# Seven products of quarters in the last layer's up-projection, two of their weight sums added by the DMA, and modulation work and token differences respaced

## The chip, the core and the metric

One core of one Trainium2 chip runs the whole program; the other cores are idle. The metric is the device time of one execution in microseconds, as the median over several runs. PE is TensorE, the matmul engine; PEld its weight loads; DVE is VectorE, ACT is ScalarE, POOL is GpSimd and SP is SyncE, which here only issues DMAs.

## What is computed

Two layers (DEPTH = 2) of a hybrid block run on 512 latent tokens and 256 context tokens, 1024 features wide. The second layer needs the context only for its keys, values and states, so everything behind its mixing works on the 512 latent tokens alone. Cut to what matters here:

```python
mod_x = silu(c) @ w_mod[l] + b_mod[l]            # 6 x 1024 numbers; mod_c the same from c_ctx
sh1, sc1, gt1, sh2, sc2, gt2 = split(mod_x, 6)
h = rmsnorm(x, g1) * (1 + sc1) + sh1
x = x + gt1 * (concat(conv(h), window_attention(h), gla(h)) @ w_out)
h = rmsnorm(x, g2) * (1 + sc2) + sh2
a, b = split(h @ w_up, 2)                        # w_up: 1024 x 5632, so a and b are 2816 wide
x = x + gt2 * ((silu(a) * b) @ w_down)           # the FFN; then the context the same in layer 0
```

Everything is float32 in and out.

## The kernel before

**Precision.** Each float32 operand of a large matmul is split into a high part (a cast on ACT) and a low part (a subtraction on DVE), and each product is three matmul passes, high by high, high by low and low by high. In the program's names `whi` and `wlo` are tiles that hold split weights (or, in the units below, one tile that holds both halves), `act` are tiles of the split tokens, `raw` is a weight slot as it was loaded, `t` is a temporary, `main` and `bank` are PSUM banks.

**Weights.** A list `plan`, written out ahead (L424 to L494), holds every weight load of the kernel in order: keys such as ("o2", m) for the out-projection, ("a", f) and ("b", f) for the two 1024 x 128 pieces of the up-projection that make 128 features f of the FFN (f = 0 to 21), ("d", bi, m) for the down-projection of block bi. SP loads them (`w_load`, L505, DMA at L519) into a ring of four slots of 512 KB; a load waits until the slot's former content has been read. `w_advance` (L523) splits weights ahead of their use, and `w_next` (L555) hands them out.

**Modulation.** The rows of `w_mod` go through the same ring, as items that `mod_items` (L362) scatters between the others: (layer, group, ...) for 12 groups of 512 features in each layer. Groups 4 to 8 of layer 0 are items (half, kk) of four matmuls each on TensorE (`mod_step`, L639, `bank<-raw,cst`), and a group ends with a copy, four transposes and a sum. All later groups are items q on VectorE (`mod_step_v`, L673): for each of two rows of an item, a multiply-add over 512 columns (`t<-raw,cst,t`) per condition, and after the fourth item a transpose, a sum and a small matmul per condition. There are two conditions (tokens and context), but only one where the last layer needs the tokens alone (its groups 4 to 11).

**The order of instructions.** A planner keeps an estimate of each engine's clock. The main line of the program issues matmuls, and whenever the estimated PE clock passes a task's ready time, that task's next step is issued (`S.poll`, L294). The engines then run their queues in that order. What an engine has been given first it does first, whatever waits behind it.

**The FFN** (L1910 on) runs in blocks of f (`F_BLOCKS`: 5, 5, 4, 4, 4 in layer 0 and 6, 6, 6, 4 in layer 1): the up-projection of the block's f, then the block's share of the down-projection, m = 0 to 7. The features f = 0 and 1 come from `Firsts` (L768), which starts while the norm of the tokens is still being made.

In layer 0 the other twenty f are `Unit`s (L1073). The weights of f and the tokens are each cut into two by two quarters, and seven products of sums of quarters (p1 to p7, table `SEVEN`, L1069) take the place of eight: with the row of `a` as first weight row, the row of `b` as second, and the left and right half of the tokens as columns. A product is 4 x 3 = 12 matmuls over half the tokens (384 columns in layer 0). The sums of token quarters (t1 to t4) are made once per layer by `Quartered.differences` (L1039), the sums of weight quarters (s1 to s4) per f by `Unit.make` (L1082) on VectorE, each followed by its split. `run_units` (L1192) makes a product's weights when the product four places ahead of it has run, and `Opened` (L740) starts the first two down-projections before the last f is ready. `Firsts.run` calls `hook`, which begins the first unit, before its last part.

In layer 1 the twenty f went through `dense_pass` (L722): two passes per f, of 8 x 3 = 24 matmuls each over all 512 tokens.

## Time and profile before

| | |
|---|---|
| median of 3 runs | 1634.88 us (1633.03 to 1636.54) |
| the profiled execution, its own time | 1632.85 us |
| its span in the trace | 1630.9 us |
| granted TensorE clock, mean | 0.995 |
| PE busy | 1586.0 us, 97% of the span |
| DVE busy | 1149.9 us, 71% |
| ACT busy | 681.1 us, 42% |
| POOL busy | 35.8 us, 2% |
| moved by DMA | 168.45 MB, 103 GB/s in the mean |

Busy times are sums over an engine's instructions, where an instruction that starts before the one ahead of it has ended counts in full; distances between starts tell an engine's pace better. A span of 1630.9 us and a time of 1632.85 us leave 1.95 us around the span.

### The profile page before, as it was taken

The numbers are of one execution on the slowest core, as the hardware profiler recorded it, in microseconds if no ns is written. First come the engines' busy times: TensorE is split into PE (matmuls) and PEld (weight loads), VectorE is DVE, ScalarE is ACT, GpSimd is POOL, SyncE is SP. The second block draws the span as 40 slices with busy tenths as digits, with TensorE's granted clock in tenths as the row PEclk, the third lists the DMA queues.
The fourth block names the chain that finished last, engine by engine and source line by source line (L and its number), as shares of the span: only waits on it lengthen the run. The fifth ranks groups of instructions, "written<-read, shape, count | busy, mean of one in ns | idle before, by whom it ended". The sixth has DMA issues, their size and how long they took to land.

```text
span 1630.9 us, 26988 instructions
## 1 busy us (share of the span) xinstructions
PE 1586.0 (97%) x10786; PEld 1370.5 (84%) x10786; DVE 1149.9 (71%) x2212; ACT 681.1 (42%) x1374; POOL 35.8 (2%) x58
## 2 busy tenths in 40 slices
PE   7999999999999999999999999998999999999998
PEld 6878777887888899998989988786889888888887
DVE  5587876669899998878788676979787433333336
ACT  4445544453653243241423535455464322222224
POOL 2000000000000000000000000000000000000002
PEclk9999999999999999999999999999999999999999
DMA  9831312243223544526354332211222333233322
GB/s 260 248 102 26 92 53 78 67 168 103 80 78 111 161 117 122 162 80 193 98 158 122 87 105 68 50 39 46 77 75 77 88 93 105 84 110 91 101 80 78
DMA packets 252670, 168.45 MB, mean 103 GB/s; under 512 B 29828, under 2 KB 233088, under 8 KB 252544
## 3 DMA queue, kind: packets, MB, share of 16 engines
q1 hardware_dynamic: 248960, 155.93, 33.2%
q0 software_dynamic: 1760, 5.47, 1.1%
q10 hardware_dynamic: 1824, 5.31, 0.9%
q8 instruction: 85, 1.39, 0.4%
q14 instruction: 41, 0.34, 0.1%
HBM read 159.35 MB, written 7.34 MB: 102 GB/s over the span
## 4 chain that ended last, share of the span: by engine, by line
PE 79%; DVE 10%; ACT 2%; DMA 1%; issue 1%; SPq 0%; DVEq 0%; ACTq 0%
PE main L139 58%; PE bank L139 19%; DVE act L188 3%; PE bank L143 3%; DVE t L188 1%; DVE wlo L188 1%; DVE t L199 1%; ACT t L155 1%; DMA raw<-in_w_mod_dram 1%; DVE t L216 1%; ACT t L177 1%; DVE mx L207 1%; DVE t L193 0%; DMA raw<-in_w_out_dram 0%; ACT whi L177 0%
## 5 line engine op out<-in xcount | busy, mean ns | idle before, releaser
L139 PE MATMUL main<-act,whi 128*128 128x512 f32 (+2 forms) x2976 | 812.8, 364 | 1.8 <-ACT act L155 1.3
L139 PEld LDWEIGHTS main<-act,whi 128*128 128x128 f32 x2976 | 530.1, 189 | 83.7 <-issue 9.1
L139 PE MATMUL main<-act,wlo 128*128 128x512 f32 (+2 forms) x1728 | 547.3, 358 | 7.5 <-DVE wlo L188 6.5
L177 ACT CAST whi<-raw 128x1024 fp32r<-128x1024 f32 (+4 forms) x222 | 186.8, 841 | 426.8 <-PE main L139 357.8
L139 PEld LDWEIGHTS main<-act,wlo 128*128 128x128 f32 x1728 | 319.1, 188 | 48.7 <-DVE wlo L188 8.7
L188 DVE TENSOR_TENSOR wlo<-raw,whi 128x1024 fp32r<-128x1024 f32 (+4 forms) x162 | 171.7, 1060 | 102.8 <-ACT whi L177 99.7
L199 DVE SCALAR_TENSOR_TENSOR act<-main,mods,act 128x512 f32<-128x512 f32 (+1 forms) x166 | 101.4, 613 | 76.8 <-PE main L139 75.7
L139 PE MATMUL bank<-act,whi 128*128 128x384 f32 (+4 forms) x736 | 153.5, 319 | 0.0
L139 PE MATMUL bank<-act,wlo 128*128 128x384 f32 (+4 forms) x548 | 127.5, 328 | 2.5 <-ACT wlo L177 2.2
L139 PEld LDWEIGHTS bank<-act,whi 128*128 128x128 f32 (+1 forms) x736 | 124.5, 187 | 4.5 <-DVE whi L188 0.2
L199 DVE SCALAR_TENSOR_TENSOR t<-raw,cst,t 128x512 f32<-128x512 f32 x154 | 110.2, 745 | 9.0 <-DMA raw<-in_w_mod_dram 8.4
L139 PEld LDWEIGHTS bank<-act,wlo 128*128 128x128 f32 (+1 forms) x548 | 98.8, 189 | 6.1 <-ACT wlo L177 2.5
L155 ACT ACTIVATE t<-bank,nm 128x256 f32<-128x256 f32 (+1 forms) x144 | 69.8, 497 | 60.0 <-DVE nm L199 55.3
L188 DVE TENSOR_TENSOR t<-main,t 128x512 f32<-128x512 f32 (+2 forms) x53 | 32.7, 617 | 77.1 <-PE main L139 77.0
L139 PE MATMUL main<-act 128*128 128x256 f32 (+1 forms) x516 | 81.6, 312 | 3.8 <-ACT act L177 2.3
L139 PEld LDWEIGHTS main<-act 128*128 128x128 f32 x516 | 71.6, 193 | 10.3 <-ACT act L177 2.9
L139 PE MATMUL main<-t,whi 128*128 128x256 f32 (+1 forms) x296 | 74.3, 338 | 0.0
L177 ACT COPY t<-bank 128x512 f32<-128x512 f32 (+3 forms) x109 | 48.9, 465 | 60.0 <-PE bank L139 32.0
L188 DVE TENSOR_TENSOR t<-t,t 128x256 f32<-128x256 f32 (+4 forms) x102 | 62.3, 615 | 13.4 <-ACT t L155 12.7
L188 DVE TENSOR_TENSOR act<-t,act 128x512 fp32r<-128x512 f32 (+7 forms) x94 | 67.2, 725 | 6.3 <-ACT act L177 4.3
L188 DVE TENSOR_TENSOR act<-act 128x768 f32<-128x768 f32 (+7 forms) x84 | 65.4, 790 | 1.3 <-ACT t L177 1.1
L207 DVE TENSOR_REDUCE mx<-bank 128x2 f32<-128x512 f32 (+2 forms) x104 | 56.3, 562 | 14.2 <-PE bank L139 13.7
(158 smaller groups left out, 1770.7 us busy)
## 6 DMA issues: line engine op xcount, KB each, us to landing
raw<-in_w_mod_dram SPq DMA_DIRECT2D x92, 512.0 KB, 4.1
raw<-in_w_up_dram SPq DMA_DIRECT2D x80, 512.0 KB, 3.9
raw<-in_w_in_dram SPq DMA_DIRECT2D x26, 512.0 KB, 3.9
raw<-in_w_down_dram SPq DMA_DIRECT2D x24, 384.0 KB, 3.5
raw<-in_w_down_dram SPq DMA_DIRECT2D x32, 256.0 KB, 3.1
raw<-in_w_down_dram SPq DMA_DIRECT2D x16, 320.0 KB, 3.6
raw<-in_w_in_dram SPq DMA_DIRECT2D x16, 256.0 KB, 3.7
raw<-in_w_out_dram SPq DMA_DIRECT2D x16, 256.0 KB, 3.0
```

Of the source, the lines that this page charges most:

```text
L139: self.pin("pe", self.nc.tensor.matmul(out, lhsT, rhs, start=start, stop=stop, **kw))
L143: self.pin("pe", self.nc.tensor.transpose(out, in_, ident))
L155: ins = self.pin("act", self.nc.scalar.activation(out, in_, func, **kw))
L177: self.pin("act", self.nc.scalar.copy(out, in_))
L188: self.pin(eng, self._v(eng).tensor_tensor(out, a, b, op))
L199: self.pin(eng, self._v(eng).scalar_tensor_tensor(out, a, s, b, op0, op1))
L207: self.pin("dve", self.nc.vector.tensor_reduce(out, in_, AX.X, op))
L216: self.pin("dve", self.nc.vector.copy_predicated(out, mask, data))
```

## The change

The units of layer 0 are now used for the last layer's f = 2 to 21 too, over halves of 256 tokens. Two of the sums of weight quarters (s1, and the inner sum of s2 and s3) are then made by accumulating DMAs from POOL: one loads a quarter into a temporary, one adds a second quarter to it, one adds a quarter to a slot that SP has loaded. Layer 0's groups 10 and 11 move from VectorE to TensorE, the groups of layer 1 come in another order (4 to 11, then 0 to 3), and the items lie at other places: fewer around the out-projection, two per f up to f = 13. The token differences are started inside `Firsts.run`, and layer 1's down-projection uses `Opened`.

```diff
@@ plan @@
     mod_todo = [(0, g, half, kk) for g in range(4, 9) for half in range(2) for kk in range(2)]
-    mod_todo += [(l, g, q) for l in range(DEPTH) for g in range(0 if l else 9, 12) for q in range(4)]
+    mod_todo += [(0, 9, q) for q in range(4)]
+    mod_todo += [(0, g, half, kk) for g in range(10, 12) for half in range(2) for kk in range(2)]
+    mod_todo += [(1, g, q) for g in (*range(4, 12), *range(4)) for q in range(4)]
...
             out2_item(l, m, m >= N_OUT2)
             if l == 0 and m == 0:
-                mod_items(2)
+                mod_items(1)
...
-                    w_item((l, nm, f), 8, cols(w_up[l, :, c0:c0 + P], 8), quarters=l == 0)
+                    w_item((l, nm, f), 8, cols(w_up[l, :, c0:c0 + P], 8), quarters=True)
+                    plan[-1]["sums"] = (l, f) if l and half else None
                 if l == 0:
-                    mod_items(2 if f < 4 else 1)
+                    mod_items(2 if f < 14 else 1)
...
-                plan[-1]["late"] = l == 0 and m == 1
+                plan[-1]["late"] = m == 1
                 if l == 0 and bi < len(blocks) - 1:
-                    mod_items((0, 1, 2, 2, 1, 1, 1, 0)[m])
+                    mod_items(((0, 1, 1, 2, 1, 1, 1, 0), (0, 1, 0, 1, 0, 1, 1, 0))[bi > 1][m])
@@ w_load @@
             at["dma"] += 1
+            if not it["mod"] and it["sums"]:
+                l, f = it["sums"]
+                def quarter(i, j):
+                    c0 = (i - 1) * FF + f * P
+                    return w_up[l, (j - 1) * 512:j * 512, c0:c0 + P].rearrange("(k p) n -> p k n", p=P)
+                S.room(t3=1)
+                it["sum"] = tmp()
+                e = it["sum"][:, :512].rearrange("p (k n) -> p k n", k=4)
+                S.pin("pool", nc.gpsimd.dma_start(e, quarter(2, 1)))
+                S.pin("pool", nc.gpsimd.dma_start(e, quarter(2, 2), accum_op=ALU.add))
+                S.pin("pool", nc.gpsimd.dma_start(it["raw"][:, :4, :], quarter(1, 1), accum_op=ALU.add))
+                it["t"] += 4000.0
@@ mod_step @@
         S.acopy(ms[:, :512], pm)
+        S.last += 1000
@@ Firsts.run @@
             self.weights(3)
+            if hook:
+                hook[0]()
             part(a, 2)
...
             if hook:
-                hook()
+                hook[1]()
             part(b, 3)
@@ Unit.make @@
-            if name == "s1":
+            if name == "s1" and self.ib["sums"]:
+                e = self.ib["sum"]
+                src = e[:, :512]
+            elif name == "s1":
...
             elif name == "s2":
-                S.tt(R["a21"], R["a11"], R["a21"], ALU.add)
+                if not self.ib["sums"]:
+                    S.tt(R["a21"], R["a11"], R["a21"], ALU.add)
@@ the FFN @@
-        norm = Normed(l, V_N2, 4, 3) if last else Quartered(l, V_N2, 4, 3, n)
+        norm = Quartered(l, V_N2, 4, 3, n)
...
-                if not last:
-                    diff = S.spawn(norm.differences(("t1", "t2", "t3")), prio=-1,
-                                   when=lambda: S.clk["pe"] if norm.done.get(gb, 0) == NK else None)
+                def hook0():
+                    diff.append(S.spawn(norm.differences(("t1", "t2", "t3")), prio=-1,
+                                        when=lambda: S.clk["pe"] if norm.done.get(gb, 0) == NK else None))
                 Firsts((l, "up"), (ga, gb)).run(norm, lambda i, s, pt: evs[i % 2]("ab"[i // 2], s, pt),
-                                                None if last else hook)
+                                                (hook0, lambda: begin(range(2, f1))))
...
-            if last:
-                X = norm.X()
-                for f in range(max(f0, 2), f1):
-                    S.room(t3=1, act=1)
-                    sil = tmp()
-                    ev_ab = swiglu(sil, act_t(F32R))
-                    for nm in ("a", "b"):
-                        dense_pass([(nm, *w_next((l, nm, f)), 0)], X, sg, ev_ab)
-                    S.gave(sil)
-            else:
-                heads = []
...
             tail(keys, ts_, 5, N_DOWN, lambda s, sums: fin.append(S.spawn(final_task(s, sums), prio=-2)), (ga, gb),
-                 tiles_)
+                 tiles_, opened)
```

The differences also find other places for t1 to t3 where half the tokens are 256 (`Quartered.at`).

**The first place: VectorE in layer 0's out-projection, where the hold weights of m = 1 to 7 are split** (`act<-raw,act` is the low part of such a weight; `t<-raw,cst,t` is a modulation step; `act<-main,mods,act` adds a product to the tokens). Before:

```order
L212 STREAM_TRANSPOSE t_4579<-t_4291 128x512
L199 SCALAR_TENSOR_TENSOR t_4539<-raw,cst,t_4539 128x512
L188 TENSOR_TENSOR act<-raw,act 128x512
L207 TENSOR_REDUCE part<-t_4579 128x16
L199 SCALAR_TENSOR_TENSOR t_4540<-raw,cst,t_4540 128x512
L199 SCALAR_TENSOR_TENSOR t_4539<-raw,cst,t_4539 128x512
...
L199 SCALAR_TENSOR_TENSOR t_4540<-raw,cst,t_4540 128x512
L188 TENSOR_TENSOR act<-raw,act 128x512
```

In the change:

```order
L188 TENSOR_TENSOR act<-raw,act 128x512
L199 SCALAR_TENSOR_TENSOR act<-main,mods_136,act 128x512
L212 STREAM_TRANSPOSE t_4576<-t_4291 128x512
L199 SCALAR_TENSOR_TENSOR act<-main,mods_136,act 128x256
L207 TENSOR_REDUCE part<-t_4576 128x16
L188 TENSOR_TENSOR act<-raw,act 128x512
L212 STREAM_TRANSPOSE t_4611<-t_4292 128x512
L188 TENSOR_TENSOR act<-raw,act 128x512
L207 TENSOR_REDUCE part<-t_4611 128x16
```

Between the first and the second low part of a hold weight stood a sum and seven modulation steps; now there stand two additions to the tokens, a transpose and a sum.

**The second place: VectorE in layer 0's first block of units** (`whi<-raw,whi` and `wlo<-raw,wlo` are the low parts of a product's weights, `t<-bank,t` takes a product out of PSUM). Before:

```order
L188 TENSOR_TENSOR mods_136<-bank,bmod 128x8
L188 TENSOR_TENSOR t_5467<-bank,t_5467 128x384
L199 SCALAR_TENSOR_TENSOR t_5379<-raw,cst,t_5379 128x512
L199 SCALAR_TENSOR_TENSOR t_5380<-raw,cst,t_5380 128x512
...
L188 TENSOR_TENSOR wlo<-raw,wlo 128x512
L188 TENSOR_TENSOR t_5467<-bank,t_5467 128x384
L188 TENSOR_TENSOR t_5585<-raw 128x512
```

In the change:

```order
L188 TENSOR_TENSOR t_5453<-bank,t_5453 128x384
L188 TENSOR_TENSOR wlo<-raw,wlo 128x512
L188 TENSOR_TENSOR t_5572<-raw 128x512
L188 TENSOR_TENSOR t_5453<-bank,t_5453 128x384
L188 TENSOR_TENSOR raw<-raw 128x512
L188 TENSOR_TENSOR whi<-t_5572,whi 128x512
```

Eight modulation steps stood ahead of that low part; none stands there now.

**The third place: POOL from the last layer's up-projection on.** Nothing but the final scaling stood there. In the change, after the loads of the tokens, once for each f (L535 loads a quarter, L536 adds one to it, L537 adds one to the slot):

```order
L535 DMA t_14501<-in_w_up_dram 128x4x128
L536 DMA t_14501<-in_w_up_dram 128x4x128
L537 DMA raw<-in_w_up_dram 128x4x128
L535 DMA t_14634<-in_w_up_dram 128x4x128
L536 DMA t_14634<-in_w_up_dram 128x4x128
L537 DMA raw<-in_w_up_dram 128x4x128
```

## Rows read from the trace of the kernel before

**Rows 1.** The page: busy time of the engines that matter, and the chain of work that ended last, as shares of the span by engine.

```profile
PE 1586.0 (97%) x10786; PEld 1370.5 (84%) x10786; DVE 1149.9 (71%) x2212; ACT 681.1 (42%) x1374; POOL 35.8 (2%) x58
PE 79%; DVE 10%; ACT 2%; DMA 1%; issue 1%; SPq 0%; DVEq 0%; ACTq 0%
```

**Rows 2.** Windows: the start of the program, one unit of layer 0 (seven products of 384 columns), and layer 1's up- and down-projection. Columns: stretch, its length, busy us (and count) of PE, PEld, DVE, ACT, POOL, granted clock, share of the 16 DMA engines, GB/s.

```profile
0.00:25.00 25.00, 15.95 (x134) 12.44 (x135) 11.96 (x36) 13.75 (x29) 8.78 (x24) 0.98 1.00 269
681.00:695.56 14.56, 14.56 (x86) 14.56 (x86) 10.63 (x18) 6.35 (x12) 0.00 (x0) 1.00 0.38 109
1277.00:1600.00 323.00, 323.00 (x1452) 268.13 (x1451) 119.17 (x137) 90.23 (x114) 0.00 (x0) 1.00 0.32 93
```

**Rows 3.** PE's timeline (start us, us, engine, line, operation, out<-in, shape, count) at three widths: layer 1's up-projection with 512 columns (a pair of high-weight matmuls comes every third matmul, and from the first of these rows to the second it is 30 such turns, 90 matmuls), a stretch of 92 matmuls of 256 columns in layer 1's out-projection and what follows it, and two products of a unit with 384 columns.

```profile
1440.66 0.62 PE L139 MATMUL main<-act,whi 128*128 128x512 f32 x2
...
1461.06 0.62 PE L139 MATMUL main<-act,whi 128*128 128x512 f32 x2
...
1234.76 11.20 PE L139 MATMUL main<-act 128*128 128x256 f32 x92
1245.80 0.50 PE L139 MATMUL bank<-ones,t 128*128 128x1 f32 x4
...
682.90 2.24 PE L139 MATMUL main<-act,wlo 128*128 128x384 f32 x12
684.98 2.24 PE L139 MATMUL bank<-act,whi 128*128 128x384 f32 x12
```

**Rows 4.** PE's timeline: the stretches of layer 0's out-projection and FFN that begin with a wait. In brackets the idle time before, and what ended it.

```profile
395.92 0.73 PE L139 MATMUL main<-act 128*128 128x512 f32 x2 [1.21 <-ACT act L177]
397.15 2.99 PE L139 MATMUL main<-act 128*128 128x512 f32 x12 [0.49 <-DVE act L188]
401.25 0.73 PE L139 MATMUL main<-act 128*128 128x512 f32 x2 [1.11 <-ACT act L177]
402.98 7.20 PE L139 MATMUL main<-act 128*128 128x512 f32 x24 [0.99 <-DVE act L188]
...
483.94 0.61 PE L139 MATMUL bank<-act,wlo 128*128 128x384 f32 x2 [2.16 <-ACT wlo L177]
484.88 3.42 PE L139 MATMUL bank<-act,wlo 128*128 128x384 f32 x10 [0.33 <-DVE wlo L188]
...
500.45 0.62 PE L139 MATMUL main<-act,wlo 128*128 128x384 f32 x2 [1.05 <-ACT wlo L177]
502.85 2.02 PE L139 MATMUL main<-act,wlo 128*128 128x384 f32 x10 [1.78 <-DVE wlo L188]
...
748.13 0.50 PE L139 MATMUL main<-act,wlo 128*128 128x512 f32 x1 [1.72 <-DVE wlo L188]
...
842.30 0.50 PE L139 MATMUL main<-act,wlo 128*128 128x512 f32 x1 [1.02 <-DVE wlo L188]
```

**Rows 5.** Windows just behind the first two of these places; columns as in rows 2.

```profile
403.00:406.40 3.40, 3.40 (x9) 2.70 (x10) 2.98 (x5) 1.32 (x3) 0.00 (x0) 0.55 0.54 148
485.00:488.40 3.40, 3.40 (x12) 3.40 (x13) 3.40 (x7) 0.21 (x2) 0.00 (x0) 0.56 0.00 0
```

**Rows 6.** DVE's timeline: the runs of modulation steps ahead of the low parts that PE waits for at 402 us and 502 us, the weight sum ahead of the low part at 484 us, and the idle time in layer 1's first up-projection.

```profile
397.60 4.72 DVE L199 SCALAR_TENSOR_TENSOR t<-raw,cst,t 128x512 f32<-128x512 f32 x7
402.24 0.68 DVE L188 TENSOR_TENSOR act<-raw,act 128x512 fp32r<-128x512 f32 x1
...
481.89 0.70 DVE L212 STREAM_TRANSPOSE t<-t 128x512 f32<-128x512 f32 x1
482.52 0.65 DVE L188 TENSOR_TENSOR t<-raw 128x512 f32<-128x512 f32 x1
...
496.81 5.38 DVE L199 SCALAR_TENSOR_TENSOR t<-raw,cst,t 128x512 f32<-128x512 f32 x8
502.11 0.68 DVE L188 TENSOR_TENSOR wlo<-raw,wlo 128x512 fp32r<-128x512 f32 x1
...
1278.40 1.23 DVE L188 TENSOR_TENSOR wlo<-raw,whi 128x1024 fp32r<-128x1024 f32 x1 [6.26 <-ACT whi L177]
```

**Rows 7.** PE's timeline: one modulation item on TensorE between other matmuls, and the four transposes that end a group.

```profile
348.34 0.28 PE L139 MATMUL main<-act,wlo 128*128 128x256 f32 x1
348.55 0.64 PE L139 MATMUL bank<-raw,cst 128*32 128x256 f32 x8
349.12 1.09 PE L139 MATMUL bank<-act 128*128 128x256 f32 x6
...
354.23 1.03 PE L143 MATMUL bank<-tab,t 128*128 128x128 f32 x8
355.02 0.48 PE L139 MATMUL main<-act,whi 128*128 128x256 f32 x2
```

**Rows 8.** Groups of instructions by line and form, of 600 to 720 us (the first two) and 1240 to 1280 us (the others). Columns: busy us, mean ns of one, idle before.

```profile
L188 DVE TENSOR_TENSOR whi<-raw,whi 128x512 fp32r<-128x512 f32 x16 | 11.0, 687 | 2.1 <-ACT whi L177 1.8
L177 ACT CAST wlo<-raw 128x512 fp32r<-128x512 f32 x16 | 9.9, 622 | 5.6 <-PE main L139 2.5 <-issue 2.2 <-DVE raw L188 0.7
...
L188 DVE TENSOR_TENSOR t<-t,t 128x256 f32<-128x256 f32 x10 | 4.2, 421 | 2.3 <-ACT t L155 2.1
L155 ACT ACTIVATE t<-act 128x256 f32<-128x256 f32 x10 | 4.2, 418 | 8.0 <-DVE act L199 8.0
```

**Rows 9.** DMA issues: out<-in, queue, count, KB each, median us from issue to landing.

```profile
raw<-in_w_up_dram SPq DMA_DIRECT2D x80, 512.0 KB, 3.9
...
act<-away POOLq DMA_DIRECT2D x4, 512.0 KB, 5.2
```

More of the change, by code (lines that the diff above doesn't have):

```diff
@@ L991, in at @@
             w = self.hw
-            if name[0] == "b" or name == "t4":
+            if 3 * w <= T and name in ("t1", "t2"):
+                t, j = self.h[kk + 4 * (name == "t2")], 2
+            elif 3 * w <= T and name == "t3":
+                if kk // 3 not in self.slots:
+                    self.slots[kk // 3] = act_t(F32R)
+                t, j = self.slots[kk // 3], kk % 3
+            elif name[0] == "b" or name == "t4":
                 t, j = self.h[kk + 4 * (name in ("b21", "b22"))], int(name in ("b22", "t4"))
@@ L1043, in differences @@
                 for kk in range(4):
-                    if kk % 2 == 0:
-                        yield dict(act=int(name != "t4"))
+                    third = 3 * w <= T
+                    if kk in ((0, 3) if third else (0, 2)) and name in (("t3",) if third else ("t1", "t2", "t3")):
+                        yield dict(act=1)
                     else:
@@ L1943, in hybrid_kernel @@
                 Firsts((l, "up"), (ga, gb)).run(norm, lambda i, s, pt: evs[i % 2]("ab"[i // 2], s, pt),
-                                                None if last else hook)
+                                                (hook0, lambda: begin(range(2, f1))))
                 S.gave(*sils)
-                if not last:
-                    S.spawn(norm.differences(("t4",)), prio=-1, when=lambda: diff["ready"] if diff["done"] else None)
-            if last:
-                X = norm.X()
-                for f in range(max(f0, 2), f1):
-                    S.room(t3=1, act=1)
-                    sil = tmp()
-                    ev_ab = swiglu(sil, act_t(F32R))
-                    for nm in ("a", "b"):
-                        dense_pass([(nm, *w_next((l, nm, f)), 0)], X, sg, ev_ab)
-                    S.gave(sil)
-            else:
-                heads = []
-                def then():
-                    mod_steps()
-                    heads.append(w_next((l, "d", bi, 0)))
-                run_units(units, 2, then)
-                for u in units:
-                    ts_.append(u.out)
-                    tiles_ += u.tiles
-                opened = [Opened((0, *heads[0], 0), ts_, sg)]
-                opened.append(Opened((1, *w_next((l, "d", bi, 1)), 0), ts_, sg))
@@ new lines, in hybrid_kernel, with then @@
+                S.spawn(norm.differences(("t4",)), prio=-1, when=lambda: diff[0]["ready"] if diff[0]["done"] else None)
+            heads = []
+            def then():
+                mod_steps()
+                heads.append(w_next((l, "d", bi, 0)))
+            run_units(units, 2, then)
+            for u in units:
+                ts_.append(u.out)
+                tiles_ += u.tiles
+            ss = (ga, gb) if bi == len(blocks) - 1 else sg
+            opened = [Opened((0, *heads[0], 0), ts_, ss)]
@@ L1970, in hybrid_kernel @@
+            opened.append(Opened((1, *w_next((l, "d", bi, 1)), 0), ts_, ss))
             if bi < len(blocks) - 1:
@@ L1976, in hybrid_kernel @@
                         w = (m, *w_next((l, "d", bi, m)), 0)
-                        if not last and m == NK - 1:
+                        if m == NK - 1:
                             begin(range(*blocks[bi + 1]))
```

7 lines of the change are left out of this document (3 added, 4 removed).

## The prediction

> **What bounds the kernel now.** I read the page first. PE is busy for 1586.0 of 1630.9 us, and 79% of the chain that ended last is its own work [rows 1]; so the time falls by what PE no longer does and by what it no longer waits for, and work of DVE, ACT or POOL counts only where PE stands still for it. Then the windows: through layer 1's up- and down-projection PE is busy 323.00 of 323.00 us at full clock, with DVE at 119.17 and ACT at 90.23 [rows 2]. There the price is the number of matmuls by their pace, and two engines have room. Then PE's timeline: in layer 0 it waits five times for low parts of weights [rows 4], and DVE's timeline shows what stood ahead of them: seven and eight modulation steps in one piece [rows 6]. Behind the first two waits the granted clock is about 0.55 for 3.4 us, nearer the lower of its two levels (1.2 of 2.4 GHz), after PE had stood still in pieces [rows 5].
>
> **1. Layer 1's products.** Removed: 20 f of 48 matmuls of 512 columns, 960. Added: 20 f of 7 x 12 = 84 matmuls of 256 columns, 1680. The pace from starts: 90 matmuls of 512 columns take 1461.06 - 1440.66 = 20.40 us, 226.7 ns each; 92 of 256 take 1245.80 - 1234.76 = 11.04 us, 120.0 ns; 12 of 384 take 2.08 us, 173.3 ns [rows 3]. At 2.4 GHz a column is 1/2.4 ns, so each width costs its columns plus 13.3 ns, and twice as many narrow ones pay that twice: this is why a saving of one product in eight gives less than one eighth. 960 x 226.7 = 217.6 us go, 1680 x 120.0 = 201.6 us come: **-16.0 us**.
>
> A rule gives another saving. The Trainium skill, page TensorE: Matmul & The Clock Gate, section Back-to-back issue gap, has N/2.4 + 2.5 ns between matmuls: 215.8 and 109.2 ns here, so 207.2 and 183.4 us and an estimated -23.8 us instead. The rows disagree with it: 13.3 ns over the columns' time at all three widths [rows 3], so the measured pace stands in the sum.
>
> **2. What feeds the new products.** Per f DVE does seven low parts, two sums, and the product's low part, ten operations of 512 columns by 687 ns, and five of 256 by 421 [rows 8]: 6.87 + 2.11 = 8.98 us in 84 x 0.120 = 10.08 us of PE. ACT does eight casts of 512 (622 ns) and five operations of 256 (418): 7.07 us. With the two sums that the DMA takes over also on DVE it would be 8.98 + 2 x 0.687 = 10.35 us, more than PE needs: the DMAs are what keeps DVE under PE. Cost nothing beside PE, while DVE stays on time; the weights are made three products ahead, 3 x 12 x 0.120 = 4.32 us, where layer 0 has 6.24 us and runs a unit of 14.56 us without a gap with DVE at 10.63 [rows 2]. The load is 89% instead of 73%, so some late low parts must be expected, and at the start of the layer 16 token differences (subtraction and low part of 256 columns, 32 x 0.421 = 13.5 us of DVE) go into a stretch where DVE had 6.26 us idle [rows 6]. They are used over the seven products of the first f, so not all is due at once. Bounds: 0, if all of it fits, to 8 us, if what exceeds the idle time (7.2 us) is waited for and the units add a little. I take **+3 us**, nearer to 0 because layer 0 shows the same code without gaps.
>
> **3. The accumulating DMAs.** 60 more issues on POOL, which has nothing else there. SP's queue is not passed, but the slot that POOL adds to is needed for s2 and s3 only, six products after its load. None accumulates before, so no row prices them. The nearest: 512 KB land in 3.9 us from SP and in 5.2 us from POOL [rows 9], these are 256 KB each. Two in series and a third in their shadow are 8 us if each costs like a 3.9 us load, and their period must stay under 10.08 us, with the next f's already started while this one runs. I take **0**; the upper end is a rival below.
>
> **4. Modulation on TensorE.** Groups 10 and 11 of layer 0: eight items. One item costs PE 349.12 - 348.34 less the 0.12 us of the matmul ahead, 0.66 us; the four transposes cost 355.02 - 354.23 = 0.79 us [rows 7]. 8 x 0.66 + 2 x 0.79 = **+6.9 us**, in PE's own path. The small matmuls of the vector form that go with them are not counted (under 0.5 us). DVE loses 32 modulation steps.
>
> **5. The waits of layer 0.** First place, 396 to 403 us: 1.21 + 0.49 + 1.11 + 0.99 = 3.80 us [rows 4], and half of 3.4 us at the low clock, 1.7: 5.5 us. The order shows seven modulation steps ahead of the low part before and none now. Second place, 484 us: 2.16 + 0.33 = 2.49 and 1.7 for the clock: 4.2 us. What stood ahead was differences, a transpose and a sum [rows 6]; the differences come earlier in the queue now, and no transpose is left, but the weight sum still is: I take half, 2.1. Third place, 500 to 503 us: 1.05 + 1.78 = 2.8 us, behind eight steps (5.38 us) that are gone from there. **-10.4 us**; bounds 0 and -12.5. What is late next: the same DVE work, less 32 steps, lies in later units as two items of one condition each, about the load that one item of two conditions made. The places at 748 and 842 us (2.7 us together) keep a similar order and stay.
>
> **6. A new piece at the first block's down-projection**: eight modulation steps now stand ahead of the low part of m = 2, and they wait for slots that m = 0 and 1 give back. Eight such steps took 5.38 us; the two opened products cover most. Bounds 0 and 3, I take **+1 us**, by the 1.02 and 1.72 us that the two similar places cost [rows 4].
>
> **Sum**: -16.0 + 3 + 0 + 6.9 - 10.4 + 1 = -15.5 us. The profiled execution took 1632.85 us, so 1617.3 by its clock; it is 2.0 us under the median of the three runs, so about **1619 us** for a median.
>
> **Rivals.** All times as medians.
> - *The waits of layer 0 come back elsewhere.* DVE is the engine behind the waits and its work in layer 0 falls by only 32 steps. Then term 5 is 0: 1619.4 + 10.4, about **1630 us**. For it: the places at 748 and 842 us arise from the same kind of order. Against it: long runs in one piece are gone at two of three places.
> - *DVE paces layer 1's units.* If its 8.98 us stretch past PE's 10.08 by waits for ACT and PE, say to 10.9 us per f, 20 x 0.8 = 16 us are lost and the gain of term 1 is gone: **1635 us**, no change. For it: 4.32 us of lead. Against it: 1.1 us are free per f.
> - *The accumulating DMAs are too slow (the other side).* Place: POOL's and SP's transfers for one f. Plain ones are 2 x 0.524 + 0.262 = 1.31 MB, at the 269 GB/s that 16 busy engines reached [rows 2] 4.87 us; the two that add move 0.524 MB, 1.95 us if they cost like plain ones. They decide from the point where they cost 2.7 times that (4.87 + 5.2 = 10.08). At four times an f takes 4.87 + 7.8 = 12.67 us, 20 f 253.4 instead of 201.6 us: +51.8, **1671 us**. Against it: plain transfers use a third of the DMA engines in this stretch [rows 2]. That all queues share the same 16 engines is what the Trainium skill says too (DMA: Bandwidth & Descriptors, section SWDGE vs HWDGE vs iDMA); no run here shows what adding costs.
> - *The narrow matmuls run closer together.* If products that stay in one bank paid half of the 13.3 ns, 1680 x 6.65 ns = 11.2 us would go too: **1608 us**. Products of 384 columns in one bank paid it in full [rows 3]. The gap rule named above, taken for both widths, would give an estimated 7.8 us less than my term, 1611 us.
> - *The change of orders does nothing and terms 4 and 6 stay*, the same time as the first rival; counted there.
>
> **How the numbers follow.** Forecast 0.65, waits come back 0.17, DVE paces 0.08, DMAs too slow 0.06, closer matmuls 0.04. Low end: -16.0 + 6.9 - 12.5 + 0 + 0 = -21.6, 1613 us, and with the closer matmuls 1602; high end: with term 5 at 0 and the others at +3 and +1, 1630 us. With both tails cut to 2 in 10 the range is **1608 to 1631 us**. A measurement of this kernel tells 0.2%, 3.3 us, from no change. Faster: nearly all of the forecast and of the closer matmuls, most of the first rival, 0.83. Same: the second rival and the rest of the first, 0.09. Slower: the DMAs and high ends of the second, 0.08.
>
> **What would show it.** In the profile after: matmuls of 128x256 in layer 1's up-projection 120 ns apart and units 10.1 us apart (term 1); DVE about 9 of 10 us there, PE without idle time (2); POOL's three DMAs per f ended before their use, and no PE wait that leads to them (3); PE without waits near 400, 484 and 500 us and without a low clock behind them (5); waits elsewhere in layer 0 under 3 us together beyond those at the two later places (5, 6). Units 11 us apart would make the prediction wrong by DVE, units of 12 us and more by the DMAs, and waits of 10 us in layer 0's later units would make it wrong by term 5.

## The result, and the profile after

The changed kernel takes 1618.56 us (median of 4 runs, 1616.48 to 1620.88) beside 1634.24 us before: a ratio of 0.9911, 95% interval 0.9898 to 0.9925. The forecast was 1619 us.

Of the page after, the busy times and the chain by engine [rows 1]:

```profile
PE 1574.5 (98%) x11562; PEld 1390.8 (86%) x11562; DVE 1220.2 (76%) x2426; ACT 755.2 (47%) x1588; POOL 103.3 (6%) x118
PE 72%; DVE 11%; DMA 5%; ACT 3%; issue 2%; DVEq 0%; SPq 0%; ACTq 0%
```

PE is busy 11.5 us less and the span, 1614.4 us, is 16.5 us shorter. The chain holds 5% of DMA where it held 1%. POOL's DMAs are not the reason: of the experiments below, e2 has none of them and 5% too, and e1 and e10 have them and 1%.

To see where the time went, both traces are cut at three places that the change does not touch: a step of the gated linear attention of layer 0, the first wait for layer 1's second norm, and the last sums of squares. PE's timeline of before:

```profile
216.24 0.93 PE L139 MATMUL bank<-act 64*64 64x64 f32 x48 [0.80 <-DVE act L188]
...
1261.94 0.38 PE L139 MATMUL main<-act,whi 128*128 128x256 f32 x1 [1.11 <-ACT act L155]
...
1622.81 0.58 PE L139 MATMUL bank<-ones,t 128*128 128x1 f32 x4 [0.83 <-DVE t L188]
```

and of after:

```profile
214.80 0.93 PE L139 MATMUL bank<-act 64*64 64x64 f32 x48 [0.82 <-DVE act L188]
...
1256.55 0.39 PE L139 MATMUL main<-act,whi 128*128 128x256 f32 x1 [1.16 <-ACT act L155]
...
1605.92 0.58 PE L139 MATMUL bank<-ones,t 128*128 128x1 f32 x4 [0.83 <-DVE t L188]
```

The start is 1.4 us shorter in this one trace; over all traces of this study it takes 214.8 to 217.7 us whatever the kernel, so it counts for nothing. The middle (layer 0's out-projection and FFN, layer 1's mixing) goes from 1045.70 to 1041.75 us, **-4.0**; the end (layer 1's FFN) from 360.87 to 349.37 us, **-11.5**. These two stretches are used for every run below. The middle scatters as well: it takes 1041.74 to 1043.78 us in the eight traces with the change's layer 0 and units in layer 1, and 1044.83 to 1045.70 in the three with layer 0 as before, so in the mean some 3 us lie between them, and not 4.0.

PE's waits of 0.3 us and more in layer 0's out-projection and FFN, after, where [rows 4] has before:

```profile
444.41 0.97 PE L139 MATMUL main<-act,whi 128*128 128x512 f32 x3 [0.98 <-ACT whi L177]
...
494.45 0.61 PE L139 MATMUL bank<-act,whi 128*128 128x384 f32 x2 [0.44 <-ACT whi L177]
495.40 2.02 PE L139 MATMUL bank<-act,whi 128*128 128x384 f32 x10 [0.33 <-DVE whi L188]
...
524.01 0.70 PE L139 MATMUL main<-act,whi 128*128 128x512 f32 x2 [1.99 <-DVE act L199]
...
580.39 2.00 PE L139 MATMUL bank<-act,wlo 128*128 128x384 f32 x10 [0.61 <-DVE wlo L188]
...
642.46 0.95 PE L139 MATMUL main<-act,whi 128*128 128x256 f32 x3 [0.51 <-DVE act L199]
...
699.61 0.62 PE L139 MATMUL bank<-act,whi 128*128 128x384 f32 x2 [0.67 <-DVE whi L188]
```

The places at 396 to 403, 484, 500, 748 and 842 us are gone; with the smaller ones 6.0 us of waits are left of 11.9. The clock behind the first place, where it was 0.55 [rows 5], and in layer 1's FFN (columns as in rows 2):

```profile
401.00:404.40 3.40, 3.40 (x17) 2.82 (x16) 3.05 (x6) 2.21 (x4) 0.00 (x0) 1.00 0.96 277
...
1274.00:1590.00 316.00, 315.80 (x2203) 294.06 (x2203) 211.31 (x376) 157.46 (x307) 62.18 (x56) 1.00 0.65 142
```

In layer 1's FFN DVE's share has gone from 37% to 67% and that of the DMA engines from 0.32 to 0.65, and PE still stands still for only 0.2 us. Its units, in PE's timeline:

```profile
1385.50 1.74 PE L139 MATMUL bank<-act,whi 128*128 128x256 f32 x12
1387.08 3.04 PE L139 MATMUL main<-act,wlo 128*128 128x256 f32 x24
...
1394.28 1.60 PE L139 MATMUL bank<-act,whi 128*128 128x256 f32 x12
1395.72 1.74 PE L139 MATMUL bank<-act,wlo 128*128 128x256 f32 x12
```

and the window of that unit (columns as above):

```profile
1385.50:1395.72 10.22, 10.22 (x87) 10.12 (x86) 7.96 (x16) 6.42 (x13) 3.13 (x4) 1.00 0.92 178
```

A product takes 1.44 us (1394.28 to 1395.72), 120.0 ns a matmul as forecast; but p3 takes 1.58 (1385.50 to 1387.08), and a unit 10.22 us (1385.50 to 1395.72) instead of 10.08. By the starts of PE's matmuls 12 of the twenty units have this. The view shows no wait there, since so short a one disappears in the modelled ends. DVE is busy for 7.96 of the 10.22 us, and the DMA engines' share is 0.92.

The DMAs that POOL issues in the same stretch (start, us, idle before):

```profile
1383.30 1.28 POOL L537 DMA_DIRECT2D raw<-in_w_up_dram  x1 [4.11 <-DVE wlo L188]
1384.06 1.30 POOL L535 DMA_DIRECT2D t<-in_w_up_dram  x1
1390.09 1.27 POOL L536 DMA_DIRECT2D t<-in_w_up_dram  x1 [4.73 <-DMA t<-in_w_up_dram]
1393.86 1.27 POOL L537 DMA_DIRECT2D raw<-in_w_up_dram  x1 [2.50 <-DVE t L199]
```

and how long DVE, over the whole execution, waited for the slot that POOL had added to (us in total, times, longest):

```profile
DVE raw L188 <- DMA raw<-in_w_up_dram: 2.9, 6, 0.8
```

The addition issued at 1383.30 us is what the sum s2 at 1387.89 us waited for, by 0.19 us. This chain arrives just in time; nothing of it was to be seen in the profile before.

### The profile page after: what moved, and what is told of

Read it like the earlier page. It is cut to its first block, busy times and chain, and to the rows that moved or that the text cites. A ratio compares the mean times of both kernels' runs of the same rounds, so it can differ in the third digit from the quotient of the medians.

```text
span 1614.4 us, 29190 instructions
## 1 busy us (share of the span) xinstructions
PE 1574.5 (98%) x11562; PEld 1390.8 (86%) x11562; DVE 1220.2 (76%) x2426; ACT 755.2 (47%) x1588; POOL 103.3 (6%) x118
## 4 chain that ended last, share of the span: by engine, by line
PE 72%; DVE 11%; DMA 5%; ACT 3%; issue 2%; DVEq 0%; SPq 0%; ACTq 0%
PE main L139 45%; PE bank L139 23%; DMA raw<-in_w_mod_dram 3%; DVE act L188 3%; PE bank L143 3%; DVE wlo L188 1%; DVE t L188 1%; DMA raw<-in_w_up_dram 1%; ACT t L155 1%; DVE t L199 1%; DVE t L216 1%; DVE act L199 1%; DVE mx L207 1%; ACT t L177 1%; ACT act L155 1%
## 5 line engine op out<-in xcount | busy, mean ns | idle before, releaser
L139 PE MATMUL main<-act,whi 128*128 128x512 f32 (+2 forms) x2772 | 667.3, 345 | 5.3 <-DVE act L199 2.5
L139 PEld LDWEIGHTS main<-act,whi 128*128 128x128 f32 x2772 | 460.4, 189 | 62.8 <-issue 12.0
L177 ACT CAST whi<-raw 128x512 fp32r<-128x512 f32 (+4 forms) x242 | 181.5, 751 | 292.4 <-PE main L139 200.9
L139 PE MATMUL bank<-act,whi 128*128 128x256 f32 (+4 forms) x1140 | 213.2, 309 | 1.7 <-DVE whi L188 1.0
L139 PE MATMUL bank<-act,wlo 128*128 128x256 f32 (+4 forms) x930 | 182.0, 309 | 0.6 <-DVE wlo L188 0.6
L199 DVE SCALAR_TENSOR_TENSOR act<-main,mods,act 128x256 f32<-128x256 f32 (+1 forms) x162 | 99.3, 616 | 75.7 <-PE main L139 74.0
L188 DVE TENSOR_TENSOR wlo<-raw,wlo 128x512 fp32r<-128x512 f32 x120 | 81.7, 687 | 39.5 <-ACT wlo L177 38.8
L188 DVE TENSOR_TENSOR whi<-raw,whi 128x512 fp32r<-128x512 f32 x120 | 81.4, 687 | 25.2 <-ACT whi L177 24.0
L177 ACT CAST wlo<-raw 128x512 fp32r<-128x512 f32 x120 | 74.6, 622 | 42.6 <-PE main L139 17.5
L139 PE MATMUL main<-t,whi 128*128 128x512 f32 (+1 forms) x302 | 75.9, 338 | 0.0
```

The source lines that it names most:

```text
L139: self.pin("pe", self.nc.tensor.matmul(out, lhsT, rhs, start=start, stop=stop, **kw))
L177: self.pin("act", self.nc.scalar.copy(out, in_))
L188: self.pin(eng, self._v(eng).tensor_tensor(out, a, b, op))
L199: self.pin(eng, self._v(eng).scalar_tensor_tensor(out, a, s, b, op0, op1))
```

## The experiments

Ratios are to the kernel before, with 95% intervals. "Middle" and "end" are the two stretches above: 1045.70 and 360.87 us before, 1041.75 and 349.37 after.

**Layer 1's part alone (e1).** Layer 0 as before:

```diff
-    mod_todo += [(0, 9, q) for q in range(4)]
-    mod_todo += [(0, g, half, kk) for g in range(10, 12) for half in range(2) for kk in range(2)]
-    mod_todo += [(1, g, q) for g in (*range(4, 12), *range(4)) for q in range(4)]
+    mod_todo += [(l, g, q) for l in range(DEPTH) for g in range(0 if l else 9, 12) for q in range(4)]
...
+                if not last:
+                    hook0()
                 Firsts((l, "up"), (ga, gb)).run(norm, lambda i, s, pt: evs[i % 2]("ab"[i // 2], s, pt),
-                                                (hook0, lambda: begin(range(2, f1))))
+                                                (hook0 if last else (lambda: None), lambda: begin(range(2, f1))))
```

> The change's part for the last layer alone: units of quarters for its up-projection with the sums by accumulating DMAs, layer 0's modulation items, their kinds and the start of its token differences as before. If the stages add up as the two traces have them, layer 1's stretch (from the first wait for its second norm to the final sums of squares) takes 349.4 us instead of 360.9 and nothing else moves: 11.5 us under before, about 1622.7 us, with PE's waits at 396 to 403, 484 and 500 us and the low clock there as before. The rival, that the respacing carries the gain, gives less than 6 us, 1628 us or more.

Measured: 1626.54 us, 0.9959 (0.9948 to 0.9971). Middle 1044.83, with the waits of [rows 4] back; end 353.72, 4.3 us over 349.37. So less than the sum of the stages, and the trace says where: DVE waited 4.11 us for an adding DMA, PE behind it 2.80 us, and over the next 4 us (1397.1 to 1401.1) the granted clock was 0.70 in the mean. This execution, 1624.36 us, was the fastest of its five; the others have no trace.

```profile
1395.81 0.69 DVE L188 TENSOR_TENSOR raw<-raw 128x512 f32<-128x512 f32 x1 [4.11 <-DMA raw<-in_w_up_dram]
```

**The respacing alone (e2).** Layer 1 as before.

> The change's other part alone: modulation items respaced and reordered, layer 0's groups 10 and 11 on TensorE, its token differences started inside the first pass; layer 1's up-projection as before. Stages that add up give 4.3 us under before, about 1630 us: 10.4 to 15 us of waits and low clock go, 6.4 to 6.9 us of TensorE work and some 6 us of new waits come. The rival that the respacing does nothing by itself gives 1634 us; that it carries the gain, 1624 us or less.

Measured: 1630.76 us, 0.9984 (0.9975 to 0.9993). Middle 1040.07, end 360.88. The traced execution (1626.91 us) was the fastest of twelve; over the runs the gain is 2.6 us (1.1 to 4.1), so the expected 4.3 lie just outside. The new waits in the trace are those of the change.

**The sums on VectorE (e3).**

```diff
-                    plan[-1]["sums"] = (l, f) if l and half else None
+                    plan[-1]["sums"] = None
```

> The change with the two weight sums on VectorE, as in layer 0, and no accumulating DMA. If VectorE's load decides, 10.35 us of its work per f stand against 10.08 us of PE, and units that are 10.22 us apart go to 10.4 to 10.7: 20 x 0.2 to 0.5 is 4 to 10 us over the change, 1622 to 1628 us. The rival: VectorE's operations overlap (starts of 512-column ones stand 0.61 us apart, not 0.687), so it needs about 9.1 us and the units stay at 10.2: within 2 us of the change.

Measured: 1625.08 us, 0.9948 (0.9935 to 0.9960); the end takes 353.32 us, with no wait of PE over 0.33 us. Units are 10.53 us apart in PE's timeline (one product to the same of the next f):

```profile
1382.68 1.60 PE L139 MATMUL bank<-act,wlo 128*128 128x256 f32 x12
...
1393.21 1.60 PE L139 MATMUL bank<-act,whi 128*128 128x256 f32 x12
```

DVE's longest wait in this unit, and the unit's window:

```profile
1384.59 0.69 DVE L188 TENSOR_TENSOR t<-raw 128x512 f32<-128x512 f32 x1 [1.33 <-DMA raw<-in_w_up_dram]
```

```profile
1382.68:1393.21 10.53, 10.42 (x86) 10.17 (x85) 9.15 (x18) 6.32 (x13) 0.00 (x0) 1.00 0.39 103
```

The time is the first theory's, but its reason is not seen: DVE is busy for 9.15 of the 10.53 us, as the rival counted, and stands still for 1.33 us until the weight slot is loaded. Ten such waits take 11.4 us of DVE in layer 1's FFN; in the change DVE's list has none for this sum, which it no longer makes. So DVE's work and the loads that it waits for pace the units together, and no run takes the two apart. The additions by DMA are worth 4.0 us of the end when they come in time, a third of its gain.

**Layer 0's groups 10 and 11 on VectorE (e4).**

```diff
-    mod_todo += [(0, 9, q) for q in range(4)]
-    mod_todo += [(0, g, half, kk) for g in range(10, 12) for half in range(2) for kk in range(2)]
+    mod_todo += [(0, g, q) for g in range(9, 12) for q in range(4)]
```

> The change with layer 0's groups 10 and 11 on VectorE again, at the places of the change. TensorE is spared 6.4 to 6.9 us; VectorE gets 32 steps more (32 x 0.66 = 21 us) around the out-projection and the first units. If the moved groups are what ended the waits, at least that much comes back as waits: 1618 to 1625 us. The rival, that the spacing alone ended them: 6 us under the change, about 1612 us.

Measured: 1627.43 us, 0.9966 (0.9955 to 0.9978), above the 1618 to 1625 us expected. Middle 1044.71, 3.0 us over the change although TensorE has less to do; waits are back at 400 us (1.3), 479 us (1.8), 498 to 500 us (2.9) and 585 us (2.2). The end, the same instructions in the same order as in the change, took 352.20 us here, with a late addition (3.88 us for DVE, 2.57 for PE), so the difference in time is not all the groups' doing. The rival is refuted: spacing alone leaves the waits.

**The changed kernel again (e5).**

> The changed kernel itself once more, for a second trace and a time beside the others of this call. Both theories give 14 to 15 us under before. In the trace the sum s2 of layer 1's units should again wait for the DMA that adds to the weight slot, up to 1 us where VectorE arrives early; the theory that this chain (load of the slot, then the adding DMA) is at its limit allows one late landing of 3 to 4 us that reaches PE, as in two of the runs before; the rival, that such a landing belongs to those other kernels, gives none.

Measured: 1621.16 us (six runs, 1618.00 to 1625.33), 0.9930 (0.9914 to 0.9946); that is 10.4 us under the 1631.61 of before on the same chip, and not 14 to 15. The traced execution was the slowest of the six, its end 356.10 us, with two late landings. DVE's waits for the slot, then the second late landing in its timeline:

```profile
DVE raw L188 <- DMA raw<-in_w_up_dram: 8.6, 5, 4.1
```

```profile
1490.80 0.69 DVE L188 TENSOR_TENSOR raw<-raw 128x512 f32<-128x512 f32 x1 [4.07 <-DMA raw<-in_w_up_dram]
1491.40 0.68 DVE L188 TENSOR_TENSOR whi<-t,whi 128x512 fp32r<-128x512 f32 x1
```

and PE's, with windows of the stretch (the last three columns are the granted clock, the DMA engines' share and GB/s):

```profile
1488.97 0.40 PE L139 MATMUL bank<-act,whi 128*128 128x256 f32 x2
1492.14 2.38 PE L139 MATMUL bank<-act,whi 128*128 128x256 f32 x10 [2.77 <-DVE whi L188]
```

```profile
1488.00:1490.00 2.00, 1.37 (x12) 1.17 (x10) 0.00 (x0) 0.00 (x0) 0.00 (x0) 1.00 1.32 202
1490.00:1492.00 2.00, 0.00 (x0) 0.00 (x0) 1.21 (x2) 0.42 (x1) 0.00 (x0) 1.00 1.15 335
1492.00:1496.00 4.00, 3.86 (x19) 3.86 (x20) 1.87 (x5) 1.35 (x4) 2.43 (x4) 0.57 0.17 35
```

The sum s2 waits for the addition; behind it on DVE stands the low part of s1's weights, whose data are long there; PE's p5 waits for that. The addition had been issued at 1484.02 us, when SP's load of the slot had landed, 8.3 us after its own issue (the median in layer 1's FFN is 4.8 us in the first trace). DVE stood at the sum from 1486.73 us on (1490.80 - 4.07); a landing 4.7 us after the issue, the median, would have been 2.0 us late, so half of the wait is a late issue and half a landing of 6.7 us. From 1488 us on the 16 engines were at a share of 1.15 and more, with the loads of the next f under way, so a collision with these is likely, but no run isolates it. 2.77 us of wait and 4 us at 0.57 of the clock cost some 4.5 us. The changed kernel loses this in some executions and not in others: the first trace of it was a lucky one.

**The slot of b in two loads (e6).**

```diff
-            for dst, src in it["load"](it["raw"]):
+            todo = it["load"](it["raw"])
+            if not it["mod"] and it["sums"]:
+                (dst, src), = todo
+                todo = [(dst[:, :4, :], src[:, :4, :]), (dst[:, 4:, :], src[:, 4:, :])]
+            for dst, src in todo:
                 S.pin("sp", nc.sync.dma_start(dst, src))
```

> The change with the slot of b loaded by two DMAs of 256 KB, the half that the sum is added to first, so that the adding DMA can start before the other half lands. If the chain of load and addition is what s2 waits for, its waits for a DMA in layer 1 shrink from 0.2 to 0.8 us to nothing, no late landing reaches PE, and the time falls by 0 to 3 us: 1615.5 to 1618.5 us. The rival, that the DMA engines' bandwidth is the limit, leaves waits and time as they are or makes them 1 to 2 us worse by 20 more issues on SP.

Measured: 1616.18 us (1614.55 to 1617.66), 0.9896 (0.9877 to 0.9915), beside 0.9930 for the change on the same chip; all four executions lie under all six of e5. End 349.37 us. In DVE's list of waits the one for the added slot is no longer there, and no wait of PE in layer 1's FFN leads to a DMA. So with the same bytes to move, the chain of load and addition decides: the half that is added to, issued at 1367.69 us, landed at 1371.83, the other half at 1372.77, and the addition starts by so much earlier.

**p3's low part first (e7).** In layer 1's units the low part of the product of f - 1 is put behind that of s4 (`S.low4`):

```diff
...
+                def low():
+                    ins = S.tt(lo[:, :2 * w], self.ta[:, :2 * w], hi[:, :2 * w].bitcast(F32), ALU.subtract)
+                    if self.l:
+                        S.behind(ins, S.low4)
...
```

> The change with VectorE's order swapped at one place of each unit of layer 1: the low part of p3's weights ahead of the low part of the previous f's product, and not behind it. If the 0.14 us by which units are over 10.08 us is p3 waiting for that low part, units come 10.08 us apart, 16 x 0.14 = 2.2 us less: about 1616 us. The rival, that the load of VectorE as a whole is at its limit, moves the wait to another product and leaves 10.2 us and 1618.5 us.

Measured: 1621.05 us, 0.9926 (0.9911 to 0.9941), no different from the change on the same chip: the traced execution had a late addition (issued at 1386.41 us, taken up at 1393.77; 4.68 us of PE), and its end took 354.09 us. By time alone it says nothing; e9 takes that disturbance away.

**Layer 0's differences early (e8).** `hook0()` ahead of `Firsts` for layer 0, as in e1, the rest as in the change.

> The change with layer 0's token differences started ahead of the first pass as before; everything else as in the change. If the start of the differences has a share in layer 0's stretch (807.9 us with it, 812.2 us before), the wait at 484 us (2.5 us and the low clock behind it) comes back here and the stretch takes 810 to 812 us; the rival, that the modulation items alone did it, leaves 808 us.

Measured, one execution: 1623.46 us; middle 1045.07, so 3.3 us of the 4.0 are lost (its end, 351.90, has a late landing). But not where I expected: nothing at 484 us. PE waits in the first pass, for the last weights of `Firsts`, behind which the clock falls:

```profile
449.56 0.96 PE L139 MATMUL main<-act,whi 128*128 128x512 f32 x3 [2.61 <-ACT whi L177]
```

```profile
450.00:454.00 4.00, 3.80 (x13) 2.91 (x12) 4.00 (x6) 1.58 (x4) 0.00 (x0) 0.63 0.38 120
```

The differences of tokens stood ahead of those weights; in the change they start behind them, and 0.98 us is left at this place. So in one trace of each, both halves of the respacing (groups on TensorE, e4; differences later, e8) are needed: without either the middle, 1044.71 and 1045.07 us, is nearer to before than to any trace with both.

**Both edits (e9).**

> The change with both edits of the two runs before it: the slot of b in two loads, and p3's low part ahead of the product's. If the late additions and the 0.14 us per unit are two separate losses, layer 1's stretch (first wait for its second norm to the final sums) falls from 349.4 us without a late landing to about 347.5, and the time from 0.9896 of before to about 0.9885: 1614 us beside a before of 1632. The rival, that the chain of VectorE has no slack left, leaves it at 0.990.

Measured: 1617.28 us, 0.9898 (0.9882 to 0.9915). End 347.71 us, 1.7 under the 349.37 of e6, as expected; PE's p3 at 1388.38 us takes 1.44 us now, and a unit 10.08 (1378.30 to 1388.38):

```profile
1378.30 1.60 PE L139 MATMUL bank<-act,wlo 128*128 128x256 f32 x12
...
1388.38 1.60 PE L139 MATMUL bank<-act,whi 128*128 128x256 f32 x12
1389.82 3.04 PE L139 MATMUL main<-act,wlo 128*128 128x256 f32 x24
```

The stretch shows the 0.14 us per unit to be that one low part. The time shows no gain over e6 (0.9898 and 0.9896), where 1.7 us is too little to be told.

**Layer 1's part with two loads (e10).** e1 with e6's edit.

> Layer 1's part of the change alone (modulation items and differences of layer 0 as before), with the slot of b in two loads. If the 4 us that the part alone fell short of the sum of its stages were the late additions, this gives the stage's full 11.5 us: 0.993 of before, with layer 0's waits as before. The rival, that the parts need each other, gives 0.995 to 0.996 again.

Measured: 1621.74 us (1620.79 to 1622.36), 0.9924 (0.9908 to 0.9940). Middle 1045.36, end 349.36. The parts add up: as far as one trace of each shows, what e1 fell short by was the late addition.

**The DMAs without adding (e11).**

```diff
-                S.pin("pool", nc.gpsimd.dma_start(e, quarter(2, 2), accum_op=ALU.add))
-                S.pin("pool", nc.gpsimd.dma_start(it["raw"][:, :4, :], quarter(1, 1), accum_op=ALU.add))
+                S.pin("pool", nc.gpsimd.dma_start(e, quarter(2, 2)))
+                S.pin("pool", nc.gpsimd.dma_start(it["raw"][:, :4, :], quarter(1, 1)))
```

> The change with the two additions of each f left out: the same 60 DMAs from POOL, all plain, so sums of weight quarters are missing. If adding costs the DMA engines more than loading, the 256 KB DMAs land sooner than 5.5 and 4.7 us, the late landings go and the time falls to that of the version with two loads (0.9896). If it is the chain of loads, waits and issues, whatever a DMA does, landings stay within 0.3 us, late ones of 3 to 4 us remain possible and the time stays at 0.991 to 0.993.

Measured: 1618.83 us, 0.9907 (0.9891 to 0.9923), end 349.41 us with no wait for the slot. DMA issues (KB each, median us to landing), of the change and without adding:

```profile
t<-in_w_up_dram POOLq DMA_DIRECT2D x40, 256.0 KB, 5.5
raw<-in_w_up_dram POOLq DMA_DIRECT2D x20, 256.0 KB, 4.7
```

```profile
t<-in_w_up_dram POOLq DMA_DIRECT2D x40, 256.0 KB, 4.1
raw<-in_w_up_dram POOLq DMA_DIRECT2D x20, 256.0 KB, 3.5
```

Adding costs 1.2 us of landing per 256 KB, a third more; part of this is the issue on POOL, 1.27 us each (L536, L537) and 0.75 without adding. It costs the DMA engines much more than that. POOL's queue in layer 1's FFN, 1274 to 1590 us (packets, MB, and the time of its packets as a share of the 16 engines), in the change and without adding:

```profile
q0 software_dynamic: 20448, 14.16, 30.2%
```

```profile
q0 software_dynamic: 4320, 14.16, 15.3%
```

Of the 54 DMAs in this stretch 18 are plain in the change too, 15.3 x 18/54 = 5.1%. So the 36 that add take 25.1% where 36 plain ones take 10.2%: 2.5 times the packet time for the same bytes, in 528 packets each where a plain one has 80. Landings and waits are those of the first theory; the time lies between the two predicted values and does not decide.

**s1's low part first (e12).**

```diff
...
-                S.tt(src, R["a21"], R["a22"], ALU.add)
+                ins = S.tt(src, R["a21"], R["a22"], ALU.add)
+                if self.ib["sums"]:
+                    S.behind(ins, S.low1)
...
```

`S.low1` is the low part of s1.

> The change with VectorE's order swapped at another place of each unit of layer 1: the low part of s1 (ready, from a temporary) ahead of the sum s2 that waits for the adding DMA. If what a late landing costs PE is the low part queued behind the waiting sum, p5 no longer waits 2 to 2.8 us; p6, two products (2.88 us) later, waits at most 1 us, the clock stays at its upper level, and the time goes to 0.989 to 0.991 of before. The rival, that the landing itself is what PE needs, moves the same wait to p6: 0.991 to 0.993.

Measured: 1621.50 us (six runs, 1618.90 to 1625.52), 0.9940 (0.9927 to 0.9954). My expectation fell: no gain, and the same spread as the change. The traced execution had no late landing (end 349.28 us), so what PE waits for in the slow ones, p6 as the rival has it or something else, was not seen.

## Why the prediction was right

The time came out within 1 us of the forecast, and for the most part by its steps. That it came so close is luck: two errors cancelled, and the four executions were good ones. As a ratio the forecast is 1619/1634.88 = 0.9903, inside the interval of the result; six more executions of the same kernel on another chip (e5) have 0.9914 to 0.9946, and there it lies outside, though 1621.16 us is well within the range.

**Term 1, the products (-16.0).** Right in its price: 120.0 ns per matmul of 256 columns, 1.44 us a product. The rival built on closer matmuls is refuted. The gap rule of the Trainium skill (TensorE: Matmul & The Clock Gate, section Back-to-back issue gap), N/2.4 + 2.5 ns, is given there for an isolated matmul and not for a stream with weight loads, which the prediction did not say. It would make a product an estimated 1.31 us, and this trace has 1.44.

**Term 2, what feeds them (+3).** Right in kind: low parts come late by a little. The loss without a late addition is 16.0 - 11.5 = 4.5 us. Of it 12 x 0.155 = 1.9 is p3, one low part behind another (shown by e9, which gets 1.7 back in the stretch). By PE's starts some 1.8 more lie at the first matmuls of three down-projections (0.6 us each, at 1324, 1419 and 1513 us) and some 0.8 at one product near the end of each block; no run isolates these. The load of DVE was taken too high: the forecast added up single operations to 8.98 us per f, but these overlap, and the unit shown has DVE busy for 7.96. So the remark that without the DMAs DVE would need 10.35 us, more than PE, is not what e3 shows: units come 10.53 us apart there, but with DVE busy for 9.15 and waiting for loads in between.

**Term 3, the accumulating DMAs (0): mis-sized.** The forecast weighed the period of the DMAs against 10.08 us and found it covered, and the rival took a price four times a load's. The price is 2.5 times (e11), so by the rival's own sum an f takes 4.87 + 2.5 x 1.95 = 9.7 us of 10.08, close to the 2.7 times from which the DMAs decide: the engines' share of 0.92 in the unit shown fits that, and without adding it is 0.65 in the same window.

The period holds, but the additions are also a chain of latencies, which the forecast did not add up: a slot becomes free, SP loads 512 KB, POOL issues the addition when these have landed, and this lands 4.7 us later. In the first trace DVE stood at the slot before the landing in six of twenty units, by up to 0.8 us; there is no slack. Of the seven traces with one load and additions (the change twice, e1, e4, e7, e8, e12) five have one or two landings for which DVE waits 3.3 to 5.8 us; each makes the end 2.5 to 6.4 us longer, the more where the clock falls behind PE's wait, as it did in three of six. None of the traces with two loads (e6, e9, e10) or without adding (e11) has one. So the chain and what adding costs the engines both seem to have a share, and no run weighs one against the other.

Against the version with two loads, the change loses 0.9930 - 0.9896 = 0.34%, 5.0 us between the medians, on the same chip; the first measurement, 0.9911, has less of it. The sentence on "six products after its load" should have set landing times in series against the use, not volumes against a rate.

**Term 4, modulation on TensorE (+6.9): too high.** Two items between products of 384 columns:

```profile
468.11 2.24 PE L139 MATMUL bank<-act,whi 128*128 128x384 f32 x12
470.29 1.07 PE L139 MATMUL bank<-raw,cst 128*32 128x256 f32 x16
471.29 2.35 PE L139 MATMUL bank<-act,wlo 128*128 128x384 f32 x12
473.48 0.60 PE L143 MATMUL bank<-tab,t 128*128 128x128 f32 x4
473.83 2.33 PE L139 MATMUL main<-act,whi 128*128 128x384 f32 x12
```

471.29 - 468.11 less a product's 2.08 is 1.10 us for two, 0.55 each; 473.83 - 471.29 less 2.08 is 0.46 for the four transposes. Six of the eight items come in such pairs, and two stand alone at 0.66, as forecast: 6 x 0.55 + 2 x 0.66 + 2 x 0.46 = 5.5 us. The 0.79 us for the transposes was a misreading: that row of [rows 7] holds eight, and no group ends there, since the sums that end groups stand at 330 and 375 us on DVE.

**Terms 5 and 6, waits (-10.4 + 1).** 5.9 us of waits and the low clock of [rows 5], (0.45 + 0.44) x 3.4 = 3.0 us, are gone: -8.9 against -9.4. The places differ more than the sum. The second place is gone altogether and the two later ones too, which were to stay (2.7 us); 0.98 us at 444 us and smaller ones are new. So the sign that waits elsewhere stay under 3 us together failed: all 6.0 us are at new places. The new piece at the first block's down-projection cost 1.99 us, not 1, by the mechanism forecast; in e5, e7 and e12 the clock fell behind it as well, which it did not in the first trace. DVE's timeline there:

```profile
519.00 1.54 DVE L199 SCALAR_TENSOR_TENSOR t<-raw,cst,t 128x512 f32<-128x512 f32 x2 [1.38 <-DMA raw<-in_w_mod_dram]
521.66 1.54 DVE L199 SCALAR_TENSOR_TENSOR t<-raw,cst,t 128x512 f32<-128x512 f32 x2 [1.13 <-DMA raw<-in_w_mod_dram]
523.12 0.75 DVE L199 SCALAR_TENSOR_TENSOR act<-main,mods,act 128x512 f32<-128x512 f32 x1
```

DVE waits for each slot to be loaded, and the addition at 523.12, which gives PE its bank, stands behind. That the waits come back elsewhere, the first rival, is half true: half of them do, and e4 and e8 lose most of the gain that way.

So the middle came to 5.5 - 8.9 = -3.4 (measured -4.0, forecast -2.5; the rest is within the scatter of the middle), the end to -11.5 (forecast -13), less a late addition now and then: two errors of about 1.5 us that cancelled, and one left out that a lucky execution hides.

**A version that beats both** is the change with the slot of b loaded in halves, 0.9896 (0.9877 to 0.9915) beside 0.9930 (0.9914 to 0.9946) for the change on the same chip; with p3's low part first as well it measures the same, 0.9898.

## What to carry to other kernels

Where a sum moves from an engine to DMAs, add up the latencies in series from the moment the slot is free to the first use, with what the issuing queue waits for in between; that its volume fits in the period is not enough. Cut a load so that what the next step of the chain needs lands by itself. And time such a kernel more than once: a chain that is just in time gives a good trace and a spread of runs.

## What the runs showed of the hardware

A DMA that adds 256 KB to SBUF lands 4.7 us after its issue on POOL (median of 20), a plain one of the same size at the same place 3.5 us. An adding one takes 1.27 us to issue and 2.5 times the packet time on the DMA engines, a plain one 0.75 us (e11). With the 16 engines at a share of 0.65 in layer 1's FFN, landings of 6.7 us occurred too (e1: issued at 1389.13 us, taken up at 1395.81).

In these traces the length of PE's wait did not decide alone whether the granted clock fell. PE's wait at 523 to 530 us takes 1.6 to 2.0 us in ten traces (the nine with the change's layer 0, and e8); the clock behind it was 0.57 in the mean of 4 us in e5, e7 and e12, and 1.00 in the other seven. In layer 1's FFN it was 0.57 behind 2.77 us (e5) and 1.00 behind 2.57 us (e4).
